# Row maxima of latent attention: rotary matmuls on three 32-row tiles of TensorE, keys of the second pair and maxima of the first unit moved

## The chip, the cores and the metric

The kernel runs on one core of a Trainium2 chip. The metric is the device time of one execution in microseconds (us); the kernel before was run three times on the chip without a profiler, and once more under the hardware profiler.

The engines are named as in the profile: PE is TensorE's matmul stream, PEld its weight loads, DVE is VectorE, ACT is ScalarE, POOL is GpSimd, SP the engine that issues most DMAs.

## The reference

The program is a two-layer backbone over 1024 latent tokens and 256 context tokens of width 1024. The first layer is windowed attention, the second is latent attention, where each of 16 heads has a 64-wide part ("nope") and a 32-wide rotary part whose key is shared by all heads. Only the second layer's attention is touched:

```python
s = (jnp.einsum("bqhd,bkhd->bhqk", qn, kn)            # 64 wide, per head
     + jnp.einsum("bqhd,bkd->bhqk", qr, kr)) * scale   # 32 wide, one key for all heads
p = jax.nn.softmax(s, axis=-1)
ox = jnp.einsum("bhqk,bkhd->bqhd", p, v)               # 1024 queries, 1280 keys
```

All of it is float32. The kernel splits a number into a part that TensorE takes exactly and a remainder ("hi" and "lo"), and adds several products.

## The kernel before, in words

The attention of the second layer is cut into 32 units (`UnitB`): 8 pairs of heads, 2 heads in a pair, 2 halves of 512 queries. One unit needs five steps.

* `prep` loads its queries: `n` (nope, hi and lo, copied to partitions 0-63 and 64-127), `r1` (rotary, four copies of 32 partitions) and `r2`.
* `top(b)`, b = 0 to 3, makes an approximate score of 128 queries against all 1280 keys in three PSUM banks (`psm`, banks 0 to 2) with queries on the partitions, and VectorE takes the row maximum of it (`reduce_max`, L1263). The maximum only shifts the exponent. TensorE's 128 rows are used as two tiles of 64 rows: rows 0-63 hold keys 0-511, rows 64-127 hold keys 512-1023. Four 512-wide matmuls (L1258, two nope, two rotary) do these keys, and two 256-wide ones (L1261, one nope and one rotary, both on the half `b % 2`) do the last 256 keys. The rotary operand of 64 rows is `kr1`: 32 rows of hi and 32 rows of lo.
* `shift` transposes the maxima (L1267) into bank 2 (`pm_bank`), and DVE (L1268) and ACT (L1273) write them into four extra rows of `r2`.
* `score(i)`, i = 0 to 4, makes the full scores with keys on the partitions: five passes (L1289) of two 64-row matmuls each, the fifth of 36 rows with the maxima in it; ACT then takes the exponential (`expo`, L1295), and POOL adds up denominators (L1303).
* `PV` multiplies the values (L1311); `fin`, `fin1`, `fin2` (L1340) and `fin3` (L1355) normalise and store.

The units are software pipelined. TensorE's, ACT's and VectorE's order in this stage is the order of the code, since it stands under `tc.manual_schedule`; other engines are scheduled. While unit `u` is scored, `nu.top(2)` and `nu.top(3)` of the next unit and `nnu.top(0)` and `nnu.top(1)` of the one after are made between its scores, and the `PV` of the unit before. The scores go through two double banks, `slots`, in turn.

`make_K(pair, blocks, ...)` forms the nope keys of a pair of heads from the latent (three products a block, L126 to L128; evacuation L1222 and L1220). Ahead of the first unit stand gate matmuls (`g_tile`) that have nothing to wait for; the tops of unit 0 are put between them. The keys of the second pair (heads 2 and 3) are formed in the first unit: `make_K(1, (0, 2))` between two tops of unit 1, `make_K(1, (1,))` in the middle of `score(1)`.

Of the kernel before, what the change touches and what calls it, by code (L numbers as in the profile page):

```python
# [60 lines left out]
def kernel(ctx: ExitStack, tc: tile.TileContext, t, out, dbg=None):  # L61
    nc = tc.nc
# [23 lines left out]
    def r_at(kb, *dims):  # L86
        n = int(np.prod(dims))
        return shp(R[:, int(kb * KB) : int(kb * KB) + n], *dims)
# [433 lines left out]
    qtb = [r_at(o, 2, 4, 128) for o in (0, 4, 80 + Z, 84 + Z, 108 + Z)]  # L522
# [173 lines left out]
    for k in range(0, 8, 2):  # L696
        w = shp(astage.next(), 2, 512)
        src = t["ada_w"][0, k * 128 : k * 128 + 256, 1024:1536].rearrange("(k p) n -> p k n", p=128)
# [169 lines left out]
    for ui, u in enumerate(units):  # L868
# [6 lines left out]
        nu = units[ui + 1] if ui + 1 < len(units) else None  # L875
# [197 lines left out]
    def g_tile(bi, p, half=None, bank=None):  # L1073
        c0 = blocks1[bi][1]
        W = wt1[bi]
        if half != 1:
            gps[bi] = pss() if bank is None else bank
        ps = gps[bi]
        for j in (0, 1) if half is None else (half,):
            for k in range(8):  # L1080
                mm3(
                    ps[:, j * 256 : j * 256 + 256],
                    [W[:, s, k, j * 128 : j * 128 + 128] for s in range(2)],
                    [hT1[p][:, s, k, :] for s in range(2)],
                    k == 0, k == 7,
                )
        if half == 0:
            return
        gg = ev.next()
        nc.scalar.activation(gg, ps, AF.Silu)  # L1090
        ch = (c0 - 800) // 128
        load(out=g1_d[ch : ch + 2, :, (p - 1) * 256 : p * 256].rearrange("c p n -> p c n"), in_=shp(gg, 2, 256))

    nx = norm_x(src1(4), xr, junk)
    for ti in range(NT):
        n = ti + 3
# [42 lines left out]
    Vq = f_at(34, NT, 4, 64)  # L1139
    kTb = [r_at(o, 2, 768) for o in (0, 6, 16, 22)]  # L1140
    kr1, kr2 = r_at(12, 768), (r_at(112, 512), r_at(15, 256))
    qtb = [[r_at(o, 2, 512), r_at(o1, 512), r_at(o2, 512)] for o, o1, o2 in ((28, 32, 34), (36, 40, 150), (104, 108, 110))]
    qt0 = [[r_at(o, 2, 512), r_at(o + 4, 512), r_at(o + 6, 512)] for o in (80, 88, 48)]
    Er = Ring(F, [10 + 4 * i for i in range(6)], 1024)
    accr = Ring(F, [47, 49], 512)
# [10 lines left out]
    def slot():  # L1156
        slots.reverse()
        return slots[1]

    def make_kr():  # L1160
        for n, c0 in enumerate((0, 4, 8)):
            pt = slot()[:, 0]
            cn = min(4, NT - c0)
            for c in range(cn):
                nc.tensor.transpose(pt[0:32, c * 128 : c * 128 + 128], krF[:, c0 + c, :], ident)
            w = slice(512 * (n // 2), 512 * (n // 2) + 128 * cn)
            ps = [64 * t for t in ((0, 1) if n == 2 else (n,))]
            src = pt[0:32, 0 : cn * 128]
            for p in ps:
                nc.scalar.copy(kr1[p : p + 32, w], src)  # L1170
                nc.scalar.copy(kr2[n // 2][p : p + 32], src)
            for p in ps:
                nc.vector.tensor_sub(kr1[p + 32 : p + 64, w], src, kr1[p : p + 32, w].bitcast(F32))
            yield
# [26 lines left out]
    def make_K(pair, blocks, sl):  # L1201
        for j, blk in enumerate(blocks):
            n0, n = ((0, 512), (512, 512), (1024, 256))[blk]
            ps = sl[:, j]
            for k in range(2):
                mm3(
                    ps[:, 0:n],
                    [ukK[:, s, k, pair * 128 : pair * 128 + 128] for s in range(2)],
                    [ckvT[:, s, k, n0 : n0 + n] for s in range(2)],
                    k == 0, k == 1,  # L1210
                )
        for j, blk in enumerate(blocks):
            w = slice(0, 512) if blk < 2 else slice(512, 768)
            to = [(e, 64 * t) for e in range(2) for t in ((0, 1) if blk == 2 else (blk,))]
            for lo in range(2):
                for e, p in to:
                    kt = kTb[(2 * pair + e) % 4][p : p + 64]
                    src = sl[64 * e : 64 * e + 64, j, 0 : w.stop - w.start]
                    if lo:
                        nc.vector.tensor_sub(kt[:, 1, w], src, kt[:, 0, w].bitcast(F32))  # L1220
                    else:
                        nc.scalar.copy(kt[:, 0, w], src)  # L1222
# [3 lines left out]
    class UnitB:  # L1226
# [24 lines left out]
        def top(self, b):  # L1251
            n, r1, _ = self.q
            bs = slice(b * 128, b * 128 + 128)
            pairs = ((n[:, 0, bs], self.kt[:, 0]), (r1[:, bs], kr1))
            rs = [slice(64 * t, 64 * t + 64) for t in range(2)]
            for i, (q, k) in enumerate(pairs):
                for t in range(2):
                    nc.tensor.matmul(psm[:, t], q[rs[t]], k[rs[t], 0:512], start=i == 0, stop=i == 1)  # L1258
            for i, (q, k) in enumerate(pairs):
                r = rs[b % 2]  # L1260
                nc.tensor.matmul(psm[:, 2, 0:256], q[r], k[r, 512:768], start=i == 0, stop=i == 1)  # L1261
            flat = psm.rearrange("p a b -> p (a b)")[:, 0:TOK]
            nc.vector.reduce_max(self.mx[:, 32 + b : 33 + b], flat, AX.X, negate=True)  # L1263

# [223 lines left out]
    with tc.manual_schedule(engines={E.PE, E.Activation, E.DVE}):  # L1488
        kr = make_kr()
        ones_kr()  # L1490
        next(kr)
        next(kr)
        g_tile(8, 3, 0, PB[:, 7, :])
        next(kr)
        g_tile(8, 3, 1)
        make_K(0, (0, 1), slot())
        g_tile(9, 3, 0, PB[:, 0, :])
        make_K(0, (2,), slot())
        g_tile(9, 3, 1)
        for _ in vk:  # L1500
            pass
        u0.top(0)
        g_tile(8, 4, 0, slots[0][:, 0])
        u0.top(1)
        g_tile(8, 4, 1)
        units[2].prep()
        u0.top(2)
        g_tile(9, 4, 0, slots[0][:, 1])
        u0.top(3)
        g_tile(9, 4, 1)  # L1510
        nc.scalar.activation(warm, const[:, 1:2], AF.Exp)
        u0.shift()
        u1.top(0)
        make_K(1, (0, 2), slots[1])
        u1.top(1)
        for ui, u in enumerate(units):
            pu, ppu = [units[ui - n] if ui >= n else None for n in (1, 2)]
            nu, nnu = [units[ui + n] if ui + n < NU else None for n in (1, 2)]
            if nnu and ui:
                nnu.prep()  # L1520
            if ui == 0:
                u.score(0)
                u.score(1, 0, 3)
                nu.top(2)
                u.score(1, 3, 5, hold=True)
                x = slot()
                make_K(1, (1,), x)
                nu.top(3)
                u.expo(1)
                u.score(2)  # L1530
                nu.shift()
            else:
                u.score(0, 0, 2)
                if nu:
                    nu.top(2)
                u.score(0, 2, 5)
                u.score(1, 0, 4)
                if nu:
                    nu.top(3)
                u.score(1, 4, 5, hold=True)  # L1540
                x = slot()
                if ui % 4 == 0 and u.pair < 7:
                    make_K(u.pair + 1, (0, 2), x)
                if ui % 4 == 1 and 0 < u.pair < 7:
                    make_K(u.pair + 1, (1,), x)
                if ui == NU - 2:
                    next(out_fill)
                pu.PV()
                u.expo(1)
                if ui % 4 > 1 and ui < 23 or ui > 25:  # L1550
                    next(wo_fill)
                if ui == NU - 1:
                    next(out_fill)
                pu.fin()
                if nu:
                    nu.shift()
                if ppu and ppu.e == 1:
                    ppu.fin3(x[:, 0])
                pu.fin2(x[:, 1])
                if ui % 8 == 0:  # L1560
                    pu.fin1()
                    for _ in make_V(u.pair // 2, x):
                        pass
            if nnu:
                nnu.top(0)
            if ui % 8:
                pu.fin1()
            if ui:
                u.score(2)
            u.score(3)  # L1570
            if nnu:
                nnu.top(1)
            u.score(4)
        u, pu = units[-1], units[-2]
        pu.fin3(slot()[:, 0])
        next(out_fill)
        next(out_fill)
        u.PV()
        u.fin()
        u.fin1()  # L1580
        next(out_fill)
        next(out_fill)
        u.fin2(slot()[:, 0])
        next(out_fill)
        next(out_fill)
        u.fin3(slot()[:, 0])
# [75 lines left out]
```

## Time and profile before

| what | value |
|---|---|
| three runs | 1632.29, 1632.44 (median), 1634.14 us |
| the profiled execution | 1635.18 us; its span, first to last instruction, 1633.4 us |
| mean granted TensorE clock | 0.991 of full speed |
| TensorE busy with matmuls | 1589.1 us, 97% of the span |
| VectorE, ACT, POOL busy | 920.6, 805.9, 714.2 us (56%, 49%, 44%) |
| tops of all units (L1258) | first starts at 1003.8 us of the span, last at 1509.2 us |

A busy matmul engine isn't one at its peak: matmuls overlap, and the profile's ends are modelled. What a change is worth is read from the starts of successive matmuls. In the rows, "64\*128 64x512" is a matmul with 64 rows and 128 columns of weights and 64x512 moving data. A row of the timeline has the start, the time from first start to last end, the engine, line and operation, tiles, shapes and a count of merged instructions, and in brackets how long the engine was idle before and what ended it.

### The profile page before, as it was taken

To read this page: it belongs to the slowest core of one execution; us is meant where nothing else is said; L and a number is where in the kernel's file an instruction comes from. 1 tells how busy PE (TensorE), PEld (TensorE's weight loads), DVE (VectorE), ACT (ScalarE), POOL (GpSimd) and SP (SyncE) were. 2 spreads that over 40 slices of the span, in tenths; PEclk is the share of its full clock that TensorE was granted. 3 is DMA by queue.
4 is the path that set the end of the run, shared out by engine and by line. 5 is a ranking of instruction groups with operands and counts; after the bars stand their busy time and mean duration, and the time that the engine had idled before them with its cause. 6 is when DMAs were issued, how large, how long until landed. Compare 5 with 4: busy or idle time off the path is not lost.

```text
span 1633.4 us, 27133 instructions
## 1 busy us (share of the span) xinstructions
PE 1589.1 (97%) x9938; PEld 1241.0 (76%) x9938; DVE 920.6 (56%) x1955; ACT 805.9 (49%) x1558; POOL 714.2 (44%) x722
## 2 busy tenths in 40 slices
PE   7999999999999999998999999999999999999998
PEld 3887787887878888878988999666766766766587
DVE  2515551548888888868443003566566566566354
ACT  3432222359777777777333413454555554544321
POOL 1241111115353333344233510478687688688510
PEclk8999999999999999999999999899999999999999
DMA  7447774444343333334027632213233323244151
GB/s 247 162 151 220 216 217 138 128 151 110 92 123 92 90 91 91 91 116 159 26 79 260 207 104 65 68 38 93 66 94 84 81 73 94 65 126 115 55 173 65
DMA packets 147205, 192.70 MB, mean 118 GB/s; under 512 B 13936, under 2 KB 84208, under 8 KB 147072
## 3 DMA queue, kind: packets, MB, share of 16 engines
q1 hardware_dynamic: 145456, 188.94, 38.5%
q10 hardware_dynamic: 1616, 2.04, 0.4%
q8 instruction: 78, 1.28, 0.3%
q14 instruction: 55, 0.45, 0.1%
HBM read 144.77 MB, written 46.15 MB: 117 GB/s over the span
## 4 chain that ended last, share of the span: by engine, by line
PE 84%; ACT 5%; DVE 5%; issue 2%; DMA 2%; POOL 1%; SPq 0%; ACTq 0%; POOLq 0%; DVEq 0%
PE PB L126 14%; PE PB L127 14%; PE PB L128 14%; PE PB L1289 12%; PE PB L1311 8%; PE PB L1258 5%; PE PB L621 4%; PE PB L611 3%; PE PB L583 2%; PE PB L181 2%; PE PB L584 2%; ACT arena_f L593 1%; ACT arena_r L121 1%; PE PB L1261 1%; DVE arena_r L122 1%
## 5 line engine op out<-in xcount | busy, mean ns | idle before, releaser
L126 PE MATMUL PB<-arena_r 128*128 128x512 f32 (+3 forms) x1496 | 508.4, 342 | 4.7 <-ACT arena_r L239 1.5
L127 PE MATMUL PB<-arena_r 128*128 128x512 f32 (+3 forms) x1496 | 503.8, 337 | 4.3 <-DVE arena_r L241 2.1
L128 PE MATMUL PB<-arena_r 128*128 128x512 f32 (+3 forms) x1496 | 501.6, 336 | 0.7 <-DVE arena_r L122 0.7
L1303 POOL TENSOR_TENSOR arena_f<-arena_f 128x512 f32<-128x512 f32 x252 | 328.8, 1305 | 111.2 <-ACT arena_f L1295 94.8
L126 PEld LDWEIGHTS PB<-arena_r 128*128 128x128 f32 x1496 | 283.9, 191 | 50.0 <-issue 15.0
L127 PEld LDWEIGHTS PB<-arena_r 128*128 128x128 f32 x1496 | 285.2, 191 | 34.1 <-DVE arena_r L388 3.4
L128 PEld LDWEIGHTS PB<-arena_r 128*128 128x128 f32 x1496 | 284.9, 190 | 29.2 <-DVE arena_r L122 1.3
L1263 DVE TENSOR_REDUCE arena_f<-PB 128x1 f32<-128x1280 f32 x128 | 190.3, 1487 | 119.1 <-PE PB L1261 110.2
L122 POOL TENSOR_TENSOR arena_r<-arena_f,arena_r 128x512 fp32r<-128x512 f32 x88 | 117.7, 1351 | 316.9 <-ACT arena_r L121 261.6
L1289 PE MATMUL PB<-arena_r 64*128 64x512 f32 (+1 forms) x1600 | 231.9, 394 | 2.6 <-DVE arena_r L1220 1.4
L1295 ACT ACTIVATE arena_f<-PB 128x1024 f32<-128x1024 f32 x160 | 164.3, 1027 | 126.0 <-PE PB L1289 84.5
L1289 PEld LDWEIGHTS PB<-arena_r 64*128 64x128 f32 (+1 forms) x1600 | 176.1, 186 | 28.0 <-ACT arena_f L1295 3.2
L590 DVE CUSTOM_DVE_ANT_0 arena_f<-PB,arena_f,small 128x256 f32<-128x256 f32 (+1 forms) x288 | 145.2, 523 | 25.3 <-PE PB L584 18.9
L1311 PE MATMUL PB<-arena_f 128*64 128x512 f32 x640 | 144.4, 597 | 0.0
L122 DVE TENSOR_TENSOR arena_r<-PB,arena_r 128x512 fp32r<-128x512 f32 (+1 forms) x186 | 123.3, 671 | 23.1 <-ACT arena_r L121 22.5
L593 ACT ACTIVATE arena_f<-arena_f,small 128x640 f32<-128x640 f32 (+2 forms) x160 | 119.5, 748 | 28.4 <-DVE small L592 27.1
L621 PE MATMUL PB<-arena_r 128*128 128x512 f32 x336 | 123.6, 441 | 3.5 <-ACT arena_f L632 3.3
L121 ACT CAST arena_r<-arena_f 128x512 fp32r<-128x512 f32 (+2 forms) x137 | 82.6, 610 | 86.7 <-PE PB L128 13.9
L121 ACT CAST arena_r<-PB 128x512 fp32r<-128x512 f32 (+1 forms) x186 | 104.1, 570 | 31.9 <-PE PB L611 30.8
L611 PE MATMUL PB<-ident,arena_f 128*128 128x128 f32 x672 | 111.5, 274 | 1.5 <-ACT arena_f L593 0.9
L1311 PEld LDWEIGHTS PB<-arena_f 128*64 128x64 f32 x640 | 43.1, 136 | 81.2 <-issue 80.4
L1258 PE MATMUL PB<-arena_r 64*128 64x512 f32 x512 | 99.0, 438 | 0.6 <-DVE arena_f L1263 0.6
(180 smaller groups left out, 1990.6 us busy)
## 6 DMA issues: line engine op xcount, KB each, us to landing
arena_f<-ada_w SPq DMA_DIRECT2D x47, 512.0 KB, 5.0
arena_r<-q_d SPq DMA_DIRECT2D x80, 256.0 KB, 4.0
arena_r<-qn_d SPq DMA_DIRECT2D x64, 256.0 KB, 3.7
arena_r<-qr_d SPq DMA_DIRECT2D x192, 64.0 KB, 3.2
arena_f<-a_w_in SPq DMA_DIRECT2D x40, 256.0 KB, 3.6
arena_f<-x SPq DMA_DIRECT2D x16, 512.0 KB, 5.9
g_d<-arena_f SPq DMA_DIRECT2D x32, 256.0 KB, 2.4
q_d<-arena_f SPq DMA_DIRECT2D x64, 128.0 KB, 2.4
```

What stands on the lines that cost most here:

```text
L121: nc.scalar.copy(hi, src)
L122: (lo_eng or nc.vector).tensor_sub(lo, src, hi.bitcast(F32))
L126: nc.tensor.matmul(o, ah, bh, start=first, stop=False)
L127: nc.tensor.matmul(o, al, bh, start=False, stop=False)
L128: nc.tensor.matmul(o, ah, bl, start=False, stop=last)
L621: nc.tensor.matmul(self.pv, V[:, self.chunks[ci], self.g, :], PT[:, s], start=ci == 0 and s == 0, stop=ci == self.m - 1 and s == 1,)
L1258: nc.tensor.matmul(psm[:, t], q[rs[t]], k[rs[t], 0:512], start=i == 0, stop=i == 1)
L1263: nc.vector.reduce_max(self.mx[:, 32 + b : 33 + b], flat, AX.X, negate=True)
L1289: nc.tensor.matmul(S[:, t], k[r, c : c + 128], q[r], start=j == 0, stop=j == 4)
L1295: nc.scalar.activation(E, self.S, AF.Exp)
L1303: eng.tensor_add(self.acc, self.acc, E[:, t])
L1311: nc.tensor.matmul(self.pv[p : p + 64], Vq[:, cs[t], self.h % 4, :], E[:, t], start=i == 0, stop=i == 4)
```

## The change

It has four parts.

1. `top(b)` does the rotary part with the hi rows of the key alone, on tiles of 32 rows: rows 0-31 for keys 0-511, rows 64-95 for keys 512-1023, and rows 32-63 or 96-127 for the last 256 keys, for which the hi rows are copied there (`kr3`). The three matmuls are on different rows and different banks. The nope matmul of the last 256 keys now comes last, on 64 rows. The number of matmuls in a top stays six.
2. `kr3` takes the place of the third query buffer of `qtb[1]`, which moves from 150 to 42.
3. `make_K(1, (0, 2))` and `make_K(1, (1,))` move ahead of the first unit, between gate tiles.
4. In unit 0 the tops 1 to 3 of unit 1 stand between whole scores 0 to 3, and `score(3)` comes ahead of `nu.shift()`, so that `nnu.top(0)` and `nnu.top(1)` follow each other there.

```diff
-    qtb = [... ((28, 32, 34), (36, 40, 150), (104, 108, 110))]
+    qtb = [... ((28, 32, 34), (36, 40, 42), (104, 108, 110))]
+    kr3 = r_at(150, 256)
...
                 nc.scalar.copy(kr2[n // 2][p : p + 32], src)
+                if n == 2:
+                    nc.scalar.copy(kr3[p + 32 : p + 64], src)
...
         def top(self, b):
-            pairs = ((n[:, 0, bs], self.kt[:, 0]), (r1[:, bs], kr1))
-            rs = [slice(64 * t, 64 * t + 64) for t in range(2)]
-            for i, (q, k) in enumerate(pairs):
-                for t in range(2):
-                    nc.tensor.matmul(psm[:, t], q[rs[t]], k[rs[t], 0:512], start=i == 0, stop=i == 1)
-            for i, (q, k) in enumerate(pairs):
-                r = rs[b % 2]
-                nc.tensor.matmul(psm[:, 2, 0:256], q[r], k[r, 512:768], start=i == 0, stop=i == 1)
+            q, k = n[:, 0, bs], self.kt[:, 0]
+            for t in range(2):
+                r = slice(64 * t, 64 * t + 64)
+                nc.tensor.matmul(psm[:, t], q[r], k[r, 0:512], start=True, stop=False)
+            for t in range(2):
+                r = slice(64 * t, 64 * t + 32)
+                nc.tensor.matmul(psm[:, t], r1[r, bs], kr1[r, 0:512], start=False, stop=True)
+            h = 64 * (b % 2)
+            r = slice(h + 32, h + 64)
+            nc.tensor.matmul(psm[:, 2, 0:256], r1[r, bs], kr3[r], start=True, stop=False)
+            r = slice(h, h + 64)
+            nc.tensor.matmul(psm[:, 2, 0:256], q[r], k[r, 512:768], start=False, stop=True)
...
+        make_K(1, (0, 2), slots[1])
         u0.top(0)
...
         u0.top(2)
+        make_K(1, (1,), slots[1])
         g_tile(9, 4, 0, slots[0][:, 1])
...
         u1.top(0)
-        make_K(1, (0, 2), slots[1])
-        u1.top(1)
...
             if ui == 0:
                 u.score(0)
-                u.score(1, 0, 3)
+                nu.top(1)
+                u.score(1)
                 nu.top(2)
-                u.score(1, 3, 5, hold=True)
-                x = slot()
-                make_K(1, (1,), x)
+                u.score(2)
                 nu.top(3)
-                u.expo(1)
-                u.score(2)
+                u.score(3)
                 nu.shift()
...
             if ui:
                 u.score(2)
-            u.score(3)
+                u.score(3)
```

Two places show it in the order of TensorE. The first is a unit in the steady part, from the transposes of `fin2` over `nnu.top(0)` into the scores. Before (L1340 `fin2`, L1258 and L1261 the top, L1289 scores):

```order
L1340 MATMUL PB<-ident,arena_f 128x128 x4
L1258 MATMUL PB<-arena_r 128x512 x4
L1261 MATMUL PB<-arena_r 128x256 x2
L1289 MATMUL PB<-arena_r 128x512 x20
L1258 MATMUL PB<-arena_r 128x512 x4
```

And after the change (L1347 `fin2`; L1260 nope, L1263 and L1266 the three rotary matmuls, L1268 the last nope one; L1296 scores):

```order
L1347 MATMUL PB<-ident,arena_f 128x128 x4
L1260 MATMUL PB<-arena_r 128x512 x2
L1263 MATMUL PB<-arena_r 128x512 x2
L1266 MATMUL PB<-arena_r 128x256
L1268 MATMUL PB<-arena_r 128x256
L1296 MATMUL PB<-arena_r 128x512 x20
L1260 MATMUL PB<-arena_r 128x512 x2
```

The place of the top among the scores is the same; within it the 32-row matmuls L1263 and L1266 now stand between 64-row ones.

The second is the first unit on TensorE, from the shift of unit 1 (L1267) to the first products with values. Before:

```order
L1267 MATMUL PB<-ident,arena_f 100x128
L1258 MATMUL PB<-arena_r 128x512 x4
L1261 MATMUL PB<-arena_r 128x256 x2
L1289 MATMUL PB<-arena_r 128x512 x10
L1258 MATMUL PB<-arena_r 128x512 x4
L1261 MATMUL PB<-arena_r 128x256 x2
L1289 MATMUL PB<-arena_r 128x512 x14
```

After, with the names of the other place and L1274 the shift:

```order
L1274 MATMUL PB<-ident,arena_f 100x128
L1260 MATMUL PB<-arena_r 128x512 x2
L1263 MATMUL PB<-arena_r 128x512 x2
L1266 MATMUL PB<-arena_r 128x256
L1268 MATMUL PB<-arena_r 128x256
L1260 MATMUL PB<-arena_r 128x512 x2
L1263 MATMUL PB<-arena_r 128x512 x2
L1266 MATMUL PB<-arena_r 128x256
L1268 MATMUL PB<-arena_r 128x256
L1296 MATMUL PB<-arena_r 128x512 x14
```

The ten score matmuls between the two tops of unit 2 have moved ahead of the shift.

More of the change, by code (lines that the diff above doesn't have):

```diff
@@ L1141 @@
     kr1, kr2 = r_at(12, 768), (r_at(112, 512), r_at(15, 256))
-    qtb = [[r_at(o, 2, 512), r_at(o1, 512), r_at(o2, 512)] for o, o1, o2 in ((28, 32, 34), (36, 40, 150), (104, 108, 110))]
+    qtb = [[r_at(o, 2, 512), r_at(o1, 512), r_at(o2, 512)] for o, o1, o2 in ((28, 32, 34), (36, 40, 42), (104, 108, 110))]
+    kr3 = r_at(150, 256)
     qt0 = [[r_at(o, 2, 512), r_at(o + 4, 512), r_at(o + 6, 512)] for o in (80, 88, 48)]
```

## The prediction, as it was made before the changed kernel ran

> **What bounds the kernel now.** I read the page's busy times and chain first, then windows over the attention, then the timeline of one steady unit, then the first unit.
>
> ```profile
> PE 1589.1 (97%) x9938; PEld 1241.0 (76%) x9938; DVE 920.6 (56%) x1955; ACT 805.9 (49%) x1558; POOL 714.2 (44%) x722
> ...
> PE 84%; ACT 5%; DVE 5%; issue 2%; DMA 2%; POOL 1%; SPq 0%; ACTq 0%; POOLq 0%; DVEq 0%
> ```
>
> TensorE carries the chain, so a change to its order counts unless a wait swallows it. By windows (span, then PE, PEld, DVE, ACT and POOL busy, granted clock, DMA):
>
> ```profile
> 1019.55:1048.20 28.65, 25.30 (x141) 17.45 (x139) 16.38 (x18) 13.28 (x19) 10.80 (x9) 0.82 0.35 97
> 1028.70:1035.60 6.90, 6.83 (x22) 4.56 (x22) 1.74 (x3) 1.40 (x3) 0.00 (x0) 0.52 0.62 176
> ...
> 1100.00:1400.00 300.00, 300.00 (x2089) 197.16 (x2089) 187.53 (x192) 152.22 (x198) 229.25 (x178) 1.00 0.31 85
> 1258.45:1272.63 14.18, 14.18 (x100) 8.83 (x101) 9.29 (x8) 6.96 (x8) 11.86 (x10) 1.00 0.32 85
> ```
>
> The steady units are TensorE's from end to end at full clock, 14.18 us each; POOL, the next engine, has 2.3 us to spare. The first unit (first row) is different: TensorE is idle for 3.35 us and its clock is 0.82. One unit on TensorE:
>
> ```profile
> 1258.53 0.60 PE L1340 MATMUL PB<-ident,arena_f 128*128 128x128 f32 x4
> 1259.06 0.49 PE L1258 MATMUL PB<-arena_r 64*128 64x512 f32 x2
> ...
> 1259.39 0.40 PE L1258 MATMUL PB<-arena_r 64*128 64x512 f32 x2
> 1259.63 0.28 PE L1261 MATMUL PB<-arena_r 64*128 64x256 f32 x1
> 1259.63 0.39 PE L1289 MATMUL PB<-arena_r 64*128 64x512 f32 x1
> 1259.75 0.28 PE L1261 MATMUL PB<-arena_r 64*128 64x256 f32 x1
> 1259.86 2.27 PE L1289 MATMUL PB<-arena_r 64*128 64x512 f32 x18
> 1261.94 0.40 PE L1258 MATMUL PB<-arena_r 64*128 64x512 f32 x1
> ...
> 1262.53 0.28 PE L1261 MATMUL PB<-arena_r 64*128 64x256 f32 x1
> 1262.65 1.80 PE L1289 MATMUL PB<-arena_r 64*128 64x512 f32 x14
> 1264.45 0.72 PE L1258 MATMUL PB<-arena_r 64*128 64x512 f32 x4
> ...
> 1265.13 0.28 PE L1261 MATMUL PB<-arena_r 64*128 64x256 f32 x1
> 1265.25 1.78 PE L1289 MATMUL PB<-arena_r 64*128 64x512 f32 x13
> 1266.99 0.73 PE L1258 MATMUL PB<-arena_r 64*128 64x512 f32 x4
> 1267.56 0.40 PE L1289 MATMUL PB<-arena_r 36*128 36x512 f32 x1
> ...
> 1267.80 0.39 PE L1289 MATMUL PB<-arena_r 36*128 36x512 f32 x1
> 1268.12 1.08 PE L1311 MATMUL PB<-arena_f 128*64 128x512 f32 x4
> ```
>
> Four things are read here. (1) Two 64-row matmuls on different halves run at once: nine pairs of scores (1259.86, 2.27 us, the last 0.39 long) are (2.27 - 0.39)/8 = 0.235 us apart; I use 0.23. A 256-wide one takes 0.12 (1259.63 to 1259.75). (2) The halves run on their own: at 1259.63 a score matmul starts with the first L1261 of top(0), on the half that L1261 leaves free. (3) A change of tile size is dear. The fourth transpose starts at 1258.53 + 0.60 - 0.27 = 1258.86 and streams 0.11 (the spacing of the four: (0.60 - 0.27)/3), yet the 64-row top is recorded at 1259.06, 0.09 late; and its second pair comes 0.33 later, not 0.23, so 0.10 more is lost. (4) Going from 64 rows to 64 columns (1267.80 to 1268.12) is 0.32 instead of 0.23, again 0.09, before its own weight load. The weight loads say where the 0.10 goes:
>
> ```profile
> 1258.42 0.47 PEld L1340 LDWEIGHTS PB<-ident,arena_f 128*128 128x128 f32 x4
> 1259.06 0.30 PEld L1258 LDWEIGHTS PB<-arena_r 64*128 64x128 f32 x4 [0.17 <-issue]
> ```
>
> The new tile's weights aren't loaded beside the old tile's matmuls; their load starts with the recorded start of the matmul. Within one tile size the load is hidden. So a change of size costs 0.09 + 0.10 = 0.19 us.
>
> VectorE's side, for the waits of top(2) and top(3):
>
> ```profile
> 1262.90 1.49 DVE L1263 TENSOR_REDUCE arena_f<-PB 128x1 f32<-128x1280 f32 x1 [0.64 <-PE PB L1261]
> 1265.44 1.49 DVE L1263 TENSOR_REDUCE arena_f<-PB 128x1 f32<-128x1280 f32 x1 [1.05 <-PE PB L1261]
> ```
>
> From a top's last matmul (1265.13) the maximum starts 0.31 later, takes 1.49, and the next top starts 0.06 after it (1266.99): 1.86 us. The seven score pairs between are 7 x 0.23 = 1.61 and don't fill it: top(2) and top(3) are bound by that chain.
>
> **The change part by part.** *The tops.* Removed: one of two 256-wide matmuls in a row, 0.12, as the rotary one now runs beside the two 512-wide ones. Added: tile sizes 64, 32, 64, two changes a top, each unknown here, since no 32-row matmul is in this program. Bounds: 0 (a 36-row matmul follows the 64-row ones with nothing lost: top(3)'s second pair starts at 1266.99 + 0.73 - 0.40 = 1267.32, the 36-row one 0.24 later; but both are on a 64-row half) and 0.19 (every change of size shown). Below nothing can't be, since loads within one size are already hidden. I take 0.19, because rows (3) and (4) are the nearest, two different changes with the same delay. A top bounded on both sides is then 0.23 + 0.19 + 0.23 + 0.19 + 0.12 = 0.96 instead of 0.23 + 0.23 + 0.12 + 0.12 = 0.70: +0.26.
>
> A page bears on this. The Trainium skill, "TensorEngine Tiling (Array Packing)", Tiling Modes, Key Properties, says that changing the tiling mode, as against the tile, drains TensorE, and it counts 64x128 and 32x128 as separate modes; rows (3) and (4) agree for other pairs of modes, and no row here shows this pair. By it the price stands at the upper bound.
>
> Top(2) and top(3): the chain of 1.86 from the last matmul is unchanged and what stands ahead of it grows, so +0.26 each. Top(0) and top(1): before, the 256-wide matmuls lie on rows 0-63 in one and on 64-127 in the other, and each time the scores of the free half run on (reading 2), so two tops cost a half 4 x 0.23 + 0.23 = 1.15. After, each change of size waits for both halves, so nothing evens out: 2 x 0.96 = 1.92, +0.77. Of this 0.06 is slack, since top(2) starts at 1264.45 though its chain would allow 1262.53 + 1.86 = 1264.39. A unit: 0.77 + 0.52 - 0.06 = 1.23.
>
> 29 units have all four tops in the loop: 29 x 1.23 = 35.7. The last but one has two: 0.5. The four of unit 0 stand between 128-row gate tiles, whose changes they had already: 4 x 0.26 = 1.0. POOL's 2.3 us and VectorE's idle time in each unit grow, so no other engine becomes the bound.
>
> *The first unit.* Its rows:
>
> ```profile
> 1021.03 0.50 PE L126 MATMUL PB<-arena_r 128*128 128x512 f32 x1
> ...
> 1023.12 0.28 PE L128 MATMUL PB<-arena_r 128*128 128x256 f32 x1
> ...
> 1027.24 0.96 PE L1289 MATMUL PB<-arena_r 64*128 64x512 f32 x5 [1.38 <-DVE arena_r L1220]
> 1028.77 1.22 PE L1258 MATMUL PB<-arena_r 64*128 64x512 f32 x4 [0.56 <-DVE arena_f L1263]
> ...
> 1036.43 1.43 PE L1289 MATMUL PB<-arena_r 64*128 64x512 f32 x10 [0.83 <-ACT arena_f L1295]
> 1038.34 0.32 PE L1267 MATMUL PB<-ident,arena_f 128*100 128x128 f32 x1 [0.47 <-DVE arena_f L1263]
> ...
> 1048.19 4.51 PE L1311 MATMUL PB<-arena_f 128*64 128x512 f32 x20
> ...
> 1021.95 0.62 ACT L1273 CAST arena_r<-arena_r 4x512 fp32r<-4x512 f32 x1
> ...
> 1022.72 2.71 ACT L1222 CAST arena_r<-PB 64x512 fp32r<-64x512 f32 x6 [0.16 <-PE PB L128]
> ```
>
> The keys' evacuation (2.71 us of ACT, then VectorE) and the maxima stop TensorE four times, 3.24 us in all, and 6.9 us of the stretch run at clock 0.52 (second window). From the shift (1019.55) to the first values (1048.19) are 28.6 us. After the change no keys are formed here. I count by chains: score(0)'s last pass waits for the maxima's rows (L1273 ends at 1022.57, 3.0 after the shift): 3.4 to top(1); three rounds of a top bound by its maximum, 0.94 + 1.86 = 2.8 each: 8.4; the shift and u2.top(0), whose rotary part in bank 2 waits for L1268 there: 3.4; top(1) and top(2) of unit 2: 5.6; top(3) to the values: 1.4. Sum 22.2. The keys go between gate tiles, 128 rows like them: from 1021.03 to 1023.12 + 0.12, less the 0.10 of the exposed first load, is 2.1, and six 512-wide matmuls at 0.23 are 1.4, so 3.5 us there, with ACT and VectorE free for the evacuation. That is 25.7 against 28.6, 2.9 less. Between top(0) and top(1) of unit 2 no scores are left, some 1.7 us idle after 0.6 more, which may bring the slow clock back for a few us. I take 2 less, with +1 and -6 as ends.
>
> *The rest.* Two more ACT copies of 32x256 for kr3, under 0.4 us each by L1222's pieces, lie in ACT's idle time ahead of the first top. The moved buffer is first used by unit 4, four units after its load can be issued: nothing.
>
> Sum: 35.7 + 0.5 + 1.0 - 2.0 = 35.2. The profiled execution of before took 1635.2, so it gives 1670.4; it lies 2.7 over the median of 1632.4, on which I put the same sum: 1667.6, rounded to 1668.
>
> **The rivals.** *A change between 64 and 32 rows is free* (faster). The tiles may be picked per instruction, with nothing drained and weights loaded ahead. For it: the halves already run independently. Against it: both changes of size in the unit show 0.09. Then top(2) and top(3) save 0.12 each, and top(0) and top(1) together 0.12: 0.36 a unit, 29 x 0.36 = 10.4, 0.7 for the other six tops, and the first unit 6: 1632.4 - 17 = 1615. It decides as soon as a change costs less than 0.06, half of the 0.12 saved.
>
> *Half price* (0.10 a change). The old tile drains but the new weights are already there, or the reverse. Top(2) and top(3) cost 0.08 each, top(0) and top(1) together 0.40, 0.50 a unit with the slack: 14.5, 0.5 for the others, first unit -4: 1643. Against it stands the PEld row, which starts only with the matmul.
>
> The Trainium skill, "TensorE: Matmul & The Clock Gate", Part 3, The mechanism, says that a weight load is pulled ahead of matmuls in flight where its row group doesn't conflict or it goes to the background buffer. By that rule the loads would be hidden and the time would be this rival's; the trace agrees within a tile size, not across one.
>
> *The three 32-row matmuls don't run at once* but the third queues behind: 0.12 more a top, 128 x 0.12 = 15: 1683. Nothing in the trace speaks for it; different rows and banks do run at once.
>
> **How the numbers follow.** Full price 0.70, half price 0.10, queueing on top of full price 0.02, free 0.18. The forecast is the likeliest, 1668. Its own range is 1654 to 1678: at 0.15 a change a unit costs 0.61 + 0.36 - 0.06 = 0.91, in all 26.4 + 1.2 - 6; at 0.22 it costs 0.89 + 0.64 - 0.06 = 1.47, in all 42.6 + 1.8 + 1. To hold 8 in 10 the low end goes down to include half price with its largest gain in the first unit, 1638, and the high end takes in the queueing, 1684. A measurement of this kernel can't tell less than 0.2% (3.3 us) from no change. Faster 0.18 (the free change), same 0.03 (from the cheap end of half price), slower 0.79.
>
> **What would show it.** In the profile of the changed kernel, a steady unit of 14.18 + 1.23 = 15.4 us instead of 14.18; the first rotary matmul of a top recorded 0.09 late and lengthened by 0.10, then the same at the last nope one; PEld idle by "issue" before L1263 and L1268; the three rotary matmuls within 0.01 us; clock 1.00 there. In the first unit no wait for L1220, a stretch some 6 us shorter, and 3.5 us more gate-stage time. It is wrong if L1263 follows L1260 at 0.23 (then the free rival), or if the late start shows without the long first matmul (half price).

## The result and the profile after

The changed kernel takes 1674.12 us (median of four runs, 1672.84 to 1676.15) against 1632.37 for the kernel before (median of four as well), a ratio of 1.0256 with a 95% interval of 1.0244 to 1.0268. The profiled execution took 1676.15 us, with a span of 1674.4 against 1633.4. The page's line of busy times:

```profile
PE 1628.8 (97%) x9938; PEld 1249.4 (75%) x9938; DVE 926.0 (55%) x1955; ACT 804.8 (48%) x1560; POOL 712.3 (43%) x722
```

The windows (same columns as before: span, then PE, PEld, DVE, ACT, POOL busy, granted clock, DMA). The first three windows run up to the first top, from there to the first shift, and on to the first value product. The first of them begins 1.3 us behind the first key transpose of this stage, which stands at 977.72 here (979.02 before). The next two are stretches at half clock; the last is one steady unit:

```profile
979.00:1006.01 27.01, 25.17 (x191) 23.86 (x188) 6.64 (x12) 11.71 (x25) 0.00 (x0) 1.00 0.16 49
1006.01:1026.90 20.89, 19.75 (x127) 16.60 (x127) 10.41 (x12) 3.80 (x8) 0.00 (x0) 0.92 0.25 65
1026.90:1051.67 24.77, 21.77 (x123) 14.06 (x121) 11.93 (x10) 9.46 (x11) 12.72 (x10) 0.86 0.40 116
1013.20:1016.50 3.30, 3.30 (x18) 3.30 (x17) 1.02 (x1) 0.00 (x0) 0.00 (x0) 0.50 0.01 1
1043.90:1050.60 6.70, 6.70 (x31) 5.06 (x27) 2.41 (x2) 2.05 (x2) 3.27 (x3) 0.50 0.00 0
1278.72:1294.18 15.46, 15.46 (x102) 9.13 (x100) 9.68 (x9) 6.95 (x8) 11.75 (x10) 1.00 0.29 77
```

A steady unit has gone from 14.18 to 15.46 us, still TensorE's from end to end and at full clock. Where the time comes from is seen in the starts of the value products, first and last, of after and then of before:

```profile
1051.67 4.51 PE L1318 MATMUL PB<-arena_f 128*64 128x512 f32 x20
...
1578.06 4.51 PE L1318 MATMUL PB<-arena_f 128*64 128x512 f32 x20
```

```profile
1536.98 4.51 PE L1311 MATMUL PB<-arena_f 128*64 128x512 f32 x20
```

From first to last they took 1536.98 - 1048.19 = 488.8 us, and now 526.4: 37.6 of the 41.0 us that the span grew. Another 3.5 lie ahead of the first value product (1048.19 to 1051.67); behind the last are 0.1 us less.

The tops in a steady unit of the changed kernel (L1260 nope, L1263 and L1266 rotary on 32 rows, L1268 last nope, L1296 scores), and the weight loads of the first of them:

```profile
1278.87 0.60 PE L1347 MATMUL PB<-ident,arena_f 128*128 128x128 f32 x4
1279.40 0.50 PE L1260 MATMUL PB<-arena_r 64*128 64x512 f32 x2
1279.83 0.50 PE L1263 MATMUL PB<-arena_r 32*128 32x512 f32 x2
1279.84 0.38 PE L1266 MATMUL PB<-arena_r 32*128 32x256 f32 x1
1280.26 0.38 PE L1268 MATMUL PB<-arena_r 64*128 64x256 f32 x1
1280.27 2.69 PE L1296 MATMUL PB<-arena_r 64*128 64x512 f32 x20
1282.69 0.51 PE L1260 MATMUL PB<-arena_r 64*128 64x512 f32 x2
1283.13 0.49 PE L1263 MATMUL PB<-arena_r 32*128 32x512 f32 x2
...
1283.55 0.38 PE L1268 MATMUL PB<-arena_r 64*128 64x256 f32 x1
```

```profile
1279.40 0.19 PEld L1260 LDWEIGHTS PB<-arena_r 64*128 64x128 f32 x2 [0.17 <-issue]
1279.83 0.18 PEld L1263 LDWEIGHTS PB<-arena_r 32*128 32x128 f32 x2 [0.24 <-issue]
1279.84 0.18 PEld L1266 LDWEIGHTS PB<-arena_r 32*128 32x128 f32 x1
1280.26 0.18 PEld L1268 LDWEIGHTS PB<-arena_r 64*128 64x128 f32 x1 [0.24 <-issue]
```

The three rotary matmuls do start within 0.01 us of each other. But each change of tile size shows the same two marks as the 128-to-64 change: L1263 is recorded 0.43 after L1260 instead of 0.23 (0.10 of L1260's own weight load in the open, 0.23 of stream, and 0.09 by which it starts late, called drain below), and L1268 0.43 after L1263. PEld stands idle 0.24 ahead of each, waiting for nothing else that the profile shows, and its load begins only with the matmul's recorded start. The 256-wide matmul that was saved is worth 0.12, the two changes cost 0.38.

### The profile page after: what moved, and what is told of

It is laid out like the page before. It is cut to its first block, busy times and chain, and to the rows that moved or that the text cites. A ratio compares the mean times of both kernels' runs of the same rounds, so it can differ in the third digit from the quotient of the medians.

```text
span 1674.4 us, 27102 instructions
## 1 busy us (share of the span) xinstructions
PE 1628.8 (97%) x9938; PEld 1249.4 (75%) x9938; DVE 926.0 (55%) x1955; ACT 804.8 (48%) x1560; POOL 712.3 (43%) x722
## 3 DMA queue, kind: packets, MB, share of 16 engines
q8 instruction: 78, 1.28, 0.3%
## 5 line engine op out<-in xcount | busy, mean ns | idle before, releaser
L1296 PE MATMUL PB<-arena_r 64*128 64x512 f32 (+1 forms) x1600 | 236.4, 403 | 0.5 <-ACT arena_f L1302 0.3
L1296 PEld LDWEIGHTS PB<-arena_r 64*128 64x128 f32 (+1 forms) x1600 | 182.1, 187 | 4.0 <-ACT arena_f L1302 1.8
L611 PEld LDWEIGHTS PB<-ident,arena_f 128*128 128x128 f32 x672 | 83.5, 140 | 20.7 <-ACT arena_f L593 5.5
```

Source lines behind the costliest of these rows:

```text
L611: nc.tensor.transpose(pt[:, h, :], self.Ps[h][:, ci * 128 : ci * 128 + 128], ident)
L1296: nc.tensor.matmul(S[:, t], k[r, c : c + 128], q[r], start=j == 0, stop=j == 4)
```

## The experiments

The theory after the result: 64-row and 32-row matmuls are two tile sizes, each change between them costs 0.09 us of drain and 0.10 of a weight load in the open, and this makes nearly all of the loss. (The sum of 0.19 is what the runs below test; its two parts are read from the recorded starts alone.) Rivals: the moves of keys and maxima make part of it; a matmul on fewer rows than the one ahead is slow whatever its tile; the three matmuls don't overlap; the price is one per top and not per change.

**tops_only.** The kernel before with the tops of the changed one (and `kr3` with its moved buffer); keys and maxima stay where they were.

> Only the tops on 32-row tiles (with kr3 and the moved buffer), order of the kernel before. Theory (each change between 64 and 32 rows costs 0.19 us, and this makes the slowdown): steady units as in the changed kernel, 15.47 us against 14.16; the 31 intervals between value products +37.6 us, ten tops outside them 0.26 each, in all about 1632.4 + 40 = 1672. Rival (the moved keys and maxima make a good part of the loss): under 1660.

Measured: 1677.92 us, ratio 1.0276 (1.0254 to 1.0298), an interval that overlaps the changed kernel's. Two value products in a row, of a unit with eight transposes, are 15.90 us apart; such units are 15.88 to 15.94 apart in the changed kernel and 14.59 to 14.68 in the kernel before. Here:

```profile
1258.44 4.51 PE L1318 MATMUL PB<-arena_f 128*64 128x512 f32 x20
...
1274.34 4.51 PE L1318 MATMUL PB<-arena_f 128*64 128x512 f32 x20
```

From its first value product (1051.81) to its last (1578.11) are 526.3 us, as in the changed kernel. The tops alone make the loss, and in the medians 3.8 us more than it. The total is some 6 us over what was expected, and its first unit, from shift to first value product, took 31.7 us against 28.6 before, with a granted clock of 0.78 there against 0.82; the expectation had counted 0.26 a top there and no clock.

**moves_only.** The changed kernel with the old tops, without `kr3` and its moved buffer. Against the kernel before, two of its places:

```diff
+        make_K(1, (0, 2), slots[1])
         u0.top(0)
...
         u0.top(2)
+        make_K(1, (1,), slots[1])
         g_tile(9, 4, 0, slots[0][:, 1])
```

> Only the moves of the second pair's keys and of the first unit's maxima, tops of the kernel before. Theory: steady units 14.16 us as before; the stretch up to the first value product keeps the new waits (VectorE evacuates keys ahead of the first maximum, the keys' bank waits for ACT, a slow clock twice) and loses the 0.26 of each of its ten tops: 3.5 - 2.6 = about +1 us, 1633, within 0.2% of before. Rival (the moves gain some 3 us, as the prediction counted): 1629 to 1630.

Measured: 1632.95 us, ratio 1.0004 (0.9993 to 1.0016): no change that can be told. The stretch from the key transposes over first top and first shift to the first value product, here and in the kernel before:

```profile
978.03:1006.32 28.29, 26.15 (x198) 24.50 (x196) 6.64 (x12) 12.03 (x24) 0.79 (x2) 1.00 0.15 47
1006.32:1024.94 18.62, 17.19 (x127) 15.55 (x127) 10.41 (x12) 3.80 (x8) 0.00 (x0) 1.00 0.28 72
1024.94:1045.29 20.35, 16.91 (x123) 11.45 (x121) 11.94 (x10) 9.47 (x11) 11.78 (x10) 1.00 0.49 135
```

```profile
979.02:1003.85 24.83, 23.79 (x188) 22.60 (x185) 6.64 (x12) 10.45 (x21) 0.79 (x2) 1.00 0.17 55
1003.85:1019.55 15.70, 15.70 (x121) 14.40 (x121) 5.97 (x4) 1.61 (x2) 0.00 (x0) 1.00 0.32 85
1019.55:1048.19 28.64, 25.29 (x140) 17.45 (x138) 16.37 (x18) 13.28 (x19) 10.79 (x9) 0.82 0.35 97
```

The first unit is 8.3 us shorter (20.35 for 28.64) and free of the slow clock. Of this 6.4 us are given back ahead of it: TensorE is busy for 3.85 us more (2.36 and 1.49 in the two windows), with the keys, and idle for 2.53 more (1.10 and 1.43), in two waits that weren't there before. The 1.9 us that are left in this pair of profiles don't show in the medians. Both waits, with their cause, are in the changed kernel too:

```profile
1003.72 0.50 PE L126 MATMUL PB<-arena_r 128*128 128x512 f32 x1 [1.10 <-ACT arena_f L1198]
```

```profile
1011.45 0.49 PE L1260 MATMUL PB<-arena_r 64*128 64x512 f32 x2 [1.14 <-DVE arena_f L1270]
```

```profile
1006.62 3.26 DVE L1223 TENSOR_TENSOR arena_r<-PB,arena_r 64x512 fp32r<-64x512 f32 x6 [11.77 <-ACT arena_r L1225]
1009.90 1.49 DVE L1270 TENSOR_REDUCE arena_f<-PB 128x1 f32<-128x1280 f32 x1
```

The keys of the second pair go to the bank from which ACT still copies the last values (L1198). And their evacuation, 3.26 us of VectorE, stands ahead of the first maximum in VectorE's order, so the second top of unit 0 waits for that maximum.

**rows36.** The kernel before, with the rotary pair of a top on 36 rows.

```diff
-                    nc.tensor.matmul(psm[:, t], q[rs[t]], k[rs[t], 0:512], start=i == 0, stop=i == 1)
+                    r = slice(64 * t, 64 * t + (64, 36)[i])
+                    nc.tensor.matmul(psm[:, t], q[r], k[r, 0:512], start=i == 0, stop=i == 1)
```

> The kernel before, with the two 512-wide rotary matmuls of a top on 36 rows instead of 64 (4 of the 32 lo rows stay in): fewer rows, same 64-row tiles. Theory (the tile size costs, not the number of rows): as before, 1632, no late start of the rotary pair. Rival (a matmul with other rows than the one ahead can't have its weights loaded early): 0.2 us at each rotary pair and at each 256-wide one, 1665 to 1680.

Measured: 1633.77 us, ratio 1.0007 (0.9994 to 1.002). The top from 1244.22, four 512-wide matmuls of which two have 36 rows, then the 256-wide ones and a score:

```profile
1244.22 0.74 PE L1259 MATMUL PB<-arena_r 64*128 64x512 f32 x4
1244.80 0.28 PE L1262 MATMUL PB<-arena_r 64*128 64x256 f32 x1
1244.80 0.39 PE L1290 MATMUL PB<-arena_r 64*128 64x512 f32 x1
1244.92 0.28 PE L1262 MATMUL PB<-arena_r 64*128 64x256 f32 x1
```

Nothing is late: 0.74 for the four, against 0.73 in the kernel before. 36 rows beside 64 cost nothing, so fewer rows alone are not what costs.

**pair32.** The same place with 32 for 36, so that only the rotary pair is on 32-row tiles and both 256-wide matmuls stay on 64.

> The kernel before, with the two 512-wide rotary matmuls on 32 rows and both 256-wide ones as before on 64: the two changes of tile size without the 256-wide matmul that is saved. Theory: a top of 0.23 + 0.19 + 0.23 + 0.19 + 0.12 + 0.12 = 1.08 us instead of 0.96, so 0.12 more than the tops alone at each of 128 tops: about 15 us more than they, 1687. Rival (the third 32-row matmul queues behind the other two, so nothing was saved): same time as the tops alone, 1672.

Measured: 1690.42 us, ratio 1.0348 (1.0324 to 1.0373). Its steady unit:

```profile
1283.13:1299.06 15.93, 15.93 (x101) 8.80 (x100) 9.35 (x8) 6.95 (x8) 11.77 (x10) 1.00 0.28 75
```

From 36 to 32 rows the kernel goes from 1633.8 to 1690.4 us. The weight loads of the rotary pair over the whole execution, first on 36 rows, then on 32 (count, busy us, mean ns, then us of idle PEld ahead of them):

```profile
L1259 PEld LDWEIGHTS PB<-arena_r 36*128 36x128 f32 x256 | 29.8, 190 | 0.6
L1259 PEld LDWEIGHTS PB<-arena_r 32*128 32x128 f32 x256 | 23.7, 182 | 35.1 <-issue 34.8 <-DMA arena_r<-x_d 0.2
```

At 32 rows, and not at 36, PEld stands idle ahead of the pair. A unit is 15.93 us from shift to shift, against 15.46 for the same form of unit in the changed kernel, and the 0.47 between them is 4 x 0.12. So the third 32-row matmul does run beside the others and saves its 0.12, as it should; the change pays for it with two changes of size.

**four_changes.** The tops alone, with the last nope matmul between the rotary ones.

```diff
-            nc.tensor.matmul(psm[:, 2, 0:256], r1[r, bs], kr3[r], start=True, stop=False)
-            r = slice(h, h + 64)
-            nc.tensor.matmul(psm[:, 2, 0:256], q[r], k[r, 512:768], start=False, stop=True)
+            nc.tensor.matmul(psm[:, 2, 0:256], q[h : h + 64], k[h : h + 64, 512:768], start=True, stop=False)
+            nc.tensor.matmul(psm[:, 2, 0:256], r1[r, bs], kr3[r], start=False, stop=True)
```

> The tops alone, with the last nope matmul (64 rows) put between the rotary ones: the 512-wide rotary pair, then 64 rows, then the 256-wide rotary one on 32 rows, so four changes of tile size in a top instead of two; same matmuls. Theory (the price is one per change): a top costs 2 x 0.19 + 0.12 = 0.50 us more than in the tops alone, 2.0 a unit (15.47 to about 17.5), 128 x 0.50 = 64, near 1740. Rival (the 32-row matmuls themselves are slow, or a top pays once): only the 0.12 that no longer runs beside the others, 15 us more, near 1692.

Measured: 1730.84 us (two runs), ratio 1.0604 (1.0583 to 1.0625). One top, and then the waits of PEld from 1100 to 1500 us, here and in the changed kernel (us in total, times, longest):

```profile
1253.08 0.50 PE L1260 MATMUL PB<-arena_r 64*128 64x512 f32 x2
1253.51 0.50 PE L1263 MATMUL PB<-arena_r 32*128 32x512 f32 x2
1253.94 0.38 PE L1266 MATMUL PB<-arena_r 64*128 64x256 f32 x1
1254.25 0.38 PE L1267 MATMUL PB<-arena_r 32*128 32x256 f32 x1
1254.56 0.72 PE L1295 MATMUL PB<-arena_r 64*128 64x512 f32 x4
```

```profile
PEld PB L1260 <- DVE arena_f L1269: 8.1, 42, 0.2
```

```profile
PEld PB L1260 <- DVE arena_f L1270: 17.5, 45, 0.4
```

Each of the four changes is there: 0.43, 0.43, and two of 0.31 around 256-wide matmuls of 0.12. The price is one per change. A unit is 17.09 us, 1.6 more than with the tops alone and not 2.0. The waits tell why: a top now takes so long that the maximum of the one before is nearly ready when the next one comes (0.19 us of idle PEld a wait against 0.39), so a part of the time is taken from the wait of top(2) and top(3). The starts of the tops in one unit of each (from 1235.99 us here, from 1279.40 in the changed kernel) put all of the missing 0.4 there: from top(0) to top(1) are 0.59 us more and from top(3) to the values 0.45, near the 0.50 expected, but from top(1) to top(2) only 0.30 (3.13 against 2.83) and from top(2) to top(3) only 0.29 (3.10 against 2.81).

**repaired.** The moves with the old tops, and with their waits taken away; the edit against moves_only:

```diff
-        make_K(1, (0, 2), slots[1])
         u0.top(0)
         g_tile(8, 4, 0, slots[0][:, 0])
         u0.top(1)
+        make_K(1, (0, 2), slots[1])
         g_tile(8, 4, 1)
...
-        make_K(1, (1,), slots[1])
+        make_K(1, (1,), PB[:, 7:8, :])
...
+            else:
+                u.score(4, 0, 3)
             if nnu:
                 nnu.top(1)
-            u.score(4)
+            u.score(4, 0 if ui else 3, 5)
```

> The moves alone, with their waits taken away: the second pair's keys stand one gate tile later (VectorE takes the first maximum before it evacuates keys, and the bank is free), the last keys use the values' bank, and three passes of score(4) stand between top(0) and top(1) of unit 2. Theory (the moves' gain in the first unit was given back by 1.1 + 1.1 us of new waits ahead of it): some 2 us less than the moves alone in the stretch up to the first value product, 1629 to 1631. Rival (that stretch is bound otherwise): 1633, the same as the moves alone.

Measured: 1627.96 us, ratio 0.9977 (0.9968 to 0.9986): faster than the kernel before by 0.2%, and than the changed one.

```profile
975.65:1000.48 24.83, 23.79 (x188) 22.60 (x185) 6.63 (x12) 10.43 (x21) 0.79 (x2) 1.00 0.17 53
1000.48:1019.71 19.23, 19.23 (x139) 17.40 (x139) 10.41 (x12) 5.41 (x10) 0.00 (x0) 1.00 0.27 70
1019.71:1040.05 20.34, 16.94 (x122) 11.33 (x120) 11.94 (x10) 9.47 (x11) 12.31 (x10) 1.00 0.52 135
```

TensorE is busy for all of the 19.23 us between first top and first shift; the stretch is 64.4 us against 67.3 with the moves alone and 69.2 before, 4.8 less than before where the medians differ by 4.3.

**even_tops** and **best.** The tops of the kernel before spaced 8, 8, 8, 1 score pairs apart instead of 10, 7, 7, 1; and the same on top of the repaired moves.

```diff
-                u.score(0, 0, 2)
+                u.score(0, 0, 1)
                 if nu:
                     nu.top(2)
-                u.score(0, 2, 5)
+                u.score(0, 1, 5)
...
-            u.score(3)
+            u.score(3, 0, 3)
             if nnu:
                 nnu.top(1)
+            u.score(3, 3, 5)
             u.score(4)
```

> The kernel before, with the tops spaced evenly among the scores: 8, 8, 8 and 1 score pairs behind tops 0 to 3 instead of 10, 7, 7 and 1 (top(1) two passes earlier, top(2) one). Theory (top(2) and top(3) wait 0.1 us each for the maximum chain of 1.86 us and then load weights in the open, 0.1): 0.2 to 0.4 us less a unit, 30 units, 1620 to 1626. Rival (eight pairs just meet the chain, and every top now waits): 1632 or more.

> The repaired moves and the even tops together, tops on 64 rows. Theory: the sum of both gains, 1617 to 1624.

Measured: 1638.07 us, ratio 1.0036 (1.0023 to 1.0049), and 1634.52, ratio 1.0014 (1.0005 to 1.0024). Both are slower than the theory had it. From first to last value product even_tops takes 494.8 us and best 494.7, against 488.8 before: the loss lies in the units with the moved tops. The time of even_tops is in its rival's range, but the rival's cause, more waiting for the maxima, is not what the trace shows. The waits of PEld from 1100 to 1500 us in even_tops:

```profile
PEld PB L1289 <- ACT arena_f L1295: 12.7, 25, 0.8
PEld PB L1258 <- DVE arena_f L1263: 10.7, 47, 0.5
```

The wait for the maxima has halved (19.8 us in the kernel before over the same stretch), but a new one stands beside it: with a top moved, scores come to their bank before ACT has taken the exponentials out of it. In the kernel before that wait is 0.3 us from 1060 to 1500, so the 10, 7, 7 order was keeping the two from meeting. How much of the 6.0 us this wait makes was not separated.

## Why the prediction was right, and where it was off

* *Price of a change of size, 0.19 us.* Right, and the step on which all else rests: drain and open load show at both changes of the top, 36 rows against 32 take it away or bring it (rows36, pair32), and two more changes bring two more (four_changes). "TensorEngine Tiling (Array Packing)" of the Trainium skill, Tiling Modes, Key Properties, has the rule by which this pair had to drain; the trace agrees, with 0.09 us at each change.
* *The free change, and half price.* Fallen. Nothing is loaded ahead across the change: PEld stands idle for 0.24 us up to the recorded start of the matmul. The pull-ahead rule of "TensorE: Matmul & The Clock Gate" of the Trainium skill, Part 3, The mechanism, holds in these traces within a tile size only, here as between 128 and 64 rows.
* *The third matmul queues.* Fallen: L1266 starts with L1263, and pair32 is 0.12 a top slower.
* *A steady unit, +1.23.* It came out at 1.28 (15.46 against 14.18), and 37.6 us over all intervals of value products where 36.2 were summed. Its parts came out too, by the starts of the tops in the two units shown: 0.73 from top(0) to top(2), 0.27 from top(2) to top(3) and 0.27 from top(3) to the values, where 0.71, 0.26 and 0.26 were summed.
* *The tops of unit 0, 0.26 each.* In tops_only the time from first top to first shift grows from 15.70 to 16.81, 1.1 where 1.0 was predicted.
* *The first unit, 2 us less.* This is the term that was mis-sized. With the keys and unit 0's tops, the stretch from key transposes to first value product was to be 1.0 us shorter (1.0 - 2.0); it is 73.95 us (1051.67 - 977.72) instead of 69.17, 4.8 longer. The first unit itself is shorter, by 3.9 us (24.77 against 28.64) and not by some 6. The step that failed is "with ACT and VectorE free for the evacuation": they were free on average, but in VectorE's order the keys stood ahead of the first maximum, and the bank was still ACT's. Two waits, 1.10 and 1.14 us, weren't in the sum. The slow clock was, but too small: it was allowed 0.9 us, the 2.9 counted less the 2 taken. Two stretches of 3.3 and 6.7 us at half clock cost half of that, 5.0, at most. The second also holds waits for maxima, and there two steps from maximum to maximum took 4.06 and 4.16 us where the step ahead of them took 2.82:

```profile
1040.51 1.49 DVE L1270 TENSOR_REDUCE arena_f<-PB 128x1 f32<-128x1280 f32 x1 [0.78 <-PE PB L1268]
1043.33 1.49 DVE L1270 TENSOR_REDUCE arena_f<-PB 128x1 f32<-128x1280 f32 x1 [1.33 <-PE PB L1268]
1047.39 1.49 DVE L1270 TENSOR_REDUCE arena_f<-PB 128x1 f32<-128x1280 f32 x1 [2.58 <-PE PB L1268]
1051.55 1.49 DVE L1270 TENSOR_REDUCE arena_f<-PB 128x1 f32<-128x1280 f32 x1 [2.66 <-PE PB L1268]
```

So the clock cost 2.6 us there and 1.65 in the first stretch, 4.2 by this estimate. With 2.24 of waits, and less the 0.9 allowed, that is some 5.6 of the 5.8 us by which the stretch missed its sum. Ahead of this stage the changed execution was 1.3 us early (977.72 against 979.02); executions of rows36, pair32 and even_tops, which change nothing there, are early too, by 1.1 to 2.5 us (977.93, 977.44, 976.48), so this needs nothing of the change. Together 37.6 + 4.8 - 1.3 = 41.1, against 41.0 in the spans.

## What to carry to other kernels

A smaller row tile is worth it only if enough matmuls of that size stand together: one change of tile size cost 0.19 us here, the drain and one weight load in the open. That is four fifths of a 512-wide matmul pair (0.23), and it held up both halves of the array; the saving was 0.12. Before fitting matmuls side by side, count the changes of tile size in the order of TensorE's program. Work that is moved to where engines look idle still queues: look at the order of the engine that must evacuate it, and at who owns its bank.

## What was not expected of the hardware

The clock: after the 1.14 us wait at 1011.45 the changed kernel ran at 0.50 from 1013.2 to 1016.5, and after an idle 1.58 us at 1042.05 (the prediction had 1.7 there, and a slow clock as possible), behind other waits, from 1043.9 to 1050.6. The moves alone have a wait of 1.43 us for the same maximum and stayed at 1.00 through that window:

```profile
1011.76 0.50 PE L1258 MATMUL PB<-arena_r 64*128 64x512 f32 x2 [1.43 <-DVE arena_f L1263]
```

So in these executions a wait of that length brought the slow clock once and once not. What decides it is open.
